# First input quarter and first weight blocks from DRAM arrays that are contiguous per transfer

## The chip, the cores and the metric

The kernel runs on one core of one Trainium2 chip. The metric is device time in microseconds of one execution, as the median of several runs. A second number, the span, runs from the first to the last instruction in the profile of one execution.

## The reference

One layer on a sequence of 1024 vectors of width 1024, all in float32:

```python
h = x @ w_in + b_in                       # -> xa | za | xb | zb | ga | gb, 1024 columns each
ya = RG_LRU(causal_conv4(xa)) * silu(za)
yb = MultiScalePool(xb) * silu(zb)
y  = (sigmoid(ga) * (ya @ w_proj_a) + sigmoid(gb) * (yb @ w_proj_b)) @ w_out + b_out
x  = LayerNorm(alpha * x + y)
```

Nearly all arithmetic lies in matrix products: `x @ w_in` (1024 x 1024 x 6144), the gates of the RG-LRU, the pooling mix, the two projections and the output.

## The kernel before

Each float32 operand is split into a high part in a shorter float format (a CAST on ScalarE, names ending in h) and the low rest (a subtraction on VectorE, names ending in l). A product is then three matmuls: high x high, high x low, low x high (`passes`, L454). Most products are done by a Strassen-like scheme with seven instead of eight block products; its operands are sums of blocks that VectorE and DMA prepare.

The order on every engine is set by a planner (`Plan`, L162). The code first records all operations; `order` (L252) then gives TensorE its matmuls in recorded order, and every other engine the waiting operation that is due first, by costs and due times of its own. All recorded operations are emitted from L388, so in the profile nearly everything has line 388 and is told apart by the names of its tiles.

What concerns the change is the start (L952 to L1022). Six warm-up matmuls on a tile of zeros (`ps_warm`) occupy TensorE while the first data come in. The first group of `w_in` is two blocks of columns, 0 and 1, whose product is done plainly, without the seven-product scheme; its results are the banks `ps_s`. The contraction of 1024 is cut into four quarters q = 0 to 3. Each quarter has two input tiles `xr[q][0]` and `xr[q][1]` of 128 partitions x 1024 (512 KB), loaded from the array `xq`, which the host has already arranged so that one such tile is one contiguous stretch, 4 KB per partition.

The first quarter is loaded in five pieces (`dma_x`, L978): of tile 0 columns 0 to 255, 256 to 511 and 512 to 1023, and of tile 1 its two halves. All are issued by SyncE (SP). The weights of the first group lie in tiles `w0r` (one per block, 128 x 1024). They are loaded by `dma_w0` (L971) in seven pieces: those of quarter 0 in three (64, 64 and 128 KB), issued by ScalarE (ACT), then quarter 1 and quarters 2 and 3 of each block, issued by SyncE. The source is `w_in[block]`, in which a partition has 4 KB: eight runs of 128 numbers (512 bytes), and a piece takes one, two or four of them. In a quarter the two halves kh = 0 and 1 are four runs apart, so a piece that takes both halves reads two separate runs per partition.

After that `split_w0` and `split_x` cast and subtract piece by piece, and `mm0` (L996) multiplies. On ScalarE the order is: its three DMA issues, a table load, the cast of the first input piece, the cast of the first weight piece, and so on.

Of the kernel before, what the change touches and what calls it, by code (L numbers as in the profile page):

```python
# [11 lines left out]
F32 = mybir.dt.float32  # L12
F32R = mybir.dt.float32r
# [3 lines left out]
P = 128  # L17
S = 1024
D = 1024
NK = D // P  # L20
H = 512
# [376 lines left out]


@with_exitstack  # L400
def layer_kernel(ctx: ExitStack, tc: tile.TileContext, xq, x, w_in, par, wg, w_pool, wpa, wpb, w_out, rows, out):
    nc = Plan(tc)

    def pool(name, bufs, space=None):
# [16 lines left out]
    def wt(name, dt=F32R, shape=(P, 2, H)):  # L421
        return wpool.tile(list(shape), dt, tag="w", name=name)
# [4 lines left out]
    def kt(name, dt=F32):  # L427
        return kpool.tile([P, S], dt, tag="k", name=name)

    def et(name):  # L430
        return epool.tile([P, H], F32, tag="e", name=name)

    def bank(name):
        return psum.tile([P, H], F32, tag="ps", name=name)
# [4 lines left out]
    out = Ref(result, as_strided(Ref.base, [S, D], [D, 1]))  # L439
    HALF = [slice(0, H), slice(H, S)]  # L440
    V, A = nc.vector, nc.scalar
# [8 lines left out]
    def split(raw, hi, lo):  # L450
        A.copy(hi, raw)
        V.tensor_tensor(lo, raw, hi.bitcast(F32), ALU.subtract)

    def passes(ps, w, m, first, last):  # L454
        (wh, wl), (mh, ml) = w, m
        for i, (a, b) in enumerate(((wh, mh), (wh, ml), (wl, mh))):
            nc.tensor.matmul(ps, a, b, start=first and i == 0, stop=last and i == 2, skip_group_check=True)
# [9 lines left out]
    KQ = 4  # L467
# [127 lines left out]
    order = [("G", 0)]  # L595
# [4 lines left out]
    def blocks_of(kind, c):  # L600
        if kind == "A":
            return XA + c, ZA + c
        if kind == "B":
            return XB + c, ZB + c
        sec = GA if c < 4 else GB
        return sec + c % 4, sec + c % 4 + 4
# [297 lines left out]
    def b_pool(g):  # L904
# [15 lines left out]
        if g == 1:  # L920
# [5 lines left out]
    sp, m, nl, y, z, z2, acc = (const.tile([P, 8], F32, name=n)  # L926
                                for n in ("sp", "sp_m", "sp_nl", "sp_y", "sp_z", "sp_z2", "sp_acc"))
# [28 lines left out]
    psw = bank("ps_warm")  # L956
    for i in range(WARM):
        nc.tensor.matmul(psw, warm[:, 0:P], warm, start=True, stop=True)
    first = blocks_of(*order[0])
    wr, wh, wl = [[f(f"{t}{n}") for n in range(2)] for t, f in  # L960
                  (("w0r", lambda n: wt(n, F32)), ("w0h", wt), ("w0l", wt))]

    xr = [[kt(f"xr{q}_{i}", F32) for i in range(2)] for q in range(KQ)]
    x13 = [[xt(f"x13{t}{q}") for t in "hl"] for q in range(KQ)]
    x2 = [xt(f"x2_{q}") for q in range(KQ)]
    xb = [xt(f"xb_{q}") for q in range(KQ)]

    def w0_part(t, n, a, b):
        return t[n].rearrange("p h (k m) -> p h k m", m=P)[:, :, a:b, :]

    def dma_w0(n, a, b, h=slice(0, 2)):  # L971

        (A if a == 0 else nc.sync).dma_start(w0_part(wr, n, a, b)[:, h], w_in[first[n]].rearrange("p (h k) m -> p h k m", h=2)[:, h, a:b, :])

    def split_w0(n, a, b, h=slice(0, 2)):
        split(*(w0_part(t, n, a, b)[:, h] for t in (wr, wh, wl)))

    def dma_x(q, i, sl=slice(0, S)):  # L978
        nc.sync.dma_start(xr[q][i][:, sl], xq[q, i][:, sl])


    def quarter(q, kh, h):
        if kh == h:
            return x13[q][0][:, kh, :], x13[q][1][:, kh, :]
        t = x2[q] if kh else xb[q]
        return t[:, 0, :], t[:, 1, :]
# [7 lines left out]
    ps0 = [[bank(f"ps_s{n}_{h}") for h in range(2)] for n in range(2)]  # L994

    def mm0(q, kh, h, n, cs=slice(0, H)):  # L996
        sl = slice(q * P, (q + 1) * P)
        passes(ps0[n][h][:, cs], (wh[n][:, kh, sl], wl[n][:, kh, sl]), tuple(t[:, cs] for t in quarter(q, kh, h)),
               q == 0 and kh == h and cs.start == 0, q == KQ - 1 and kh != h)


    PARTS = [slice(0, H // 2), slice(H // 2, H)]
    dma_w0(0, 0, 1, slice(0, 1))
    with nc.within(-2 * SOON):
        for sl in PARTS:
            dma_x(0, 0, sl)
    dma_w0(0, 0, 1, slice(1, 2))
    dma_w0(1, 0, 1)
    dma_x(0, 0, HALF[1])
    dma_x(0, 1, HALF[0])  # L1010
    dma_x(0, 1, HALF[1])
    dma_w0(0, 1, 2)
# [53 lines left out]
    def parts(q, n=0):  # L1066
        r = xr[q][0].rearrange("p (i s) -> p i s", i=2)
        todo = [(r, *x13[q])] + [(xr[q][raws[p][0]][:, HALF[raws[p][1]]], *quarter(q, *p)) for p in ((0, 1), (1, 0))]
        for raw, t, u in todo[n:]:
            hi(raw, t)  # L1070
        for raw, t, u in todo[n:]:
            lo(raw, t, u)
        for kh, h in ((0, 0), (1, 1), (0, 1), (1, 0)):
            for n in range(2):
                mm0(q, kh, h, n)

    def each(f, qs, *a):
        for q in qs:
            f(q, *a)

    split_w0(0, 0, 1, slice(0, 1))
    for kh, h in ((0, 0), (1, 1), (0, 1), (1, 0)):
        if kh == h == 1:
            split_w0(0, 0, 1, slice(1, 2))
        for sl in PARTS if kh == h == 0 else (slice(0, H),):
            split_x(0, kh, h, sl)
            mm0(0, kh, h, 0, sl)
        if kh == h == 1:
            split_w0(1, 0, 1)
            mm0(0, 0, 0, 1)  # L1090
        if kh or h:
            mm0(0, kh, h, 1)
# [29 lines left out]
    g = Group("A0", w.out, X, *takes0)  # L1122
# [44 lines left out]
    for i in range(1, len(order)):  # L1167
# [17 lines left out]
        if i > 1:  # L1185
            g = Group(f"{kind}{c}", W.pop(i), X, *takes)
# [170 lines left out]
    for i, (n, j) in enumerate(steps):  # L1357
# [7 lines left out]
        if j == 1:  # L1365
            a, c, m1, um = [[None] * KQ for _ in range(4)]
        X_, W_ = ([(hi_[:, k, :], lo_[:, k, :]) for hi_, lo_ in ops[i][o:o + 2] for k in range(2)] for o in (0, 2))
        for g in range(KQ):
# [5 lines left out]
            for q in range(KQ):  # L1374
                sl = slice(q * P, (q + 1) * P)
# [10 lines left out]
            if (n, j) in DONE:  # L1386
                d, h = DONE[n, j]
                d += g
                if j == 3:
                    t, u = ps, et(f"c12_{n}{g}") if n == "b" else None  # L1390
                else:
                    t = u = m1[g] if j == 2 else um[g][:, HALF[h]]
# [12 lines left out]
            if (n, j, g) in CASTS:  # L1405
                k = CASTS.index((n, j, g))
# [89 lines left out]
    a, c = ([None] * KQ for _ in range(2))  # L1496
# [25 lines left out]
    for g in range(KQ):  # L1522
        o_product(c[g], 4, g, False, True)
        o_add(4 + g, 1, c[g], -1, False, True)
        pieces = (slice(0, H),) if g < KQ - 1 else (slice(0, H // 2), slice(H // 2, H))
# [60 lines left out]
```

## Time and profile before

| | us |
|---|---|
| median of 3 runs | 740.91 (740.2 to 741.23) |
| the profiled execution | 740.07 |
| its span | 738.3 |
| TensorE busy (matmuls) | 729.5 |
| VectorE busy | 600.8 |
| ScalarE busy | 459.0 |
| GpSimd busy | 67.9 |

In the rows of the profile PE is TensorE, PEld its weight loads, DVE is VectorE, ACT ScalarE, POOL GpSimd and SP SyncE; SPq and ACTq are these engines' issues of DMAs. A timeline row has the start, the length, the engine, the line, the operation and out<-in. A bracket holds the idle time ahead of it and what ended that. Matmuls are pipelined, and their ends are modelled: the distance between starts is what one costs. `w0r<-in_w_in` is a load of weights of the first group, `xr<-in_xq` one of the input.

### The profile page before, as it was taken

The numbers are of one execution on the slowest core, as the hardware profiler recorded it, in microseconds if no ns is written. First come the engines' busy times: TensorE is split into PE (matmuls) and PEld (weight loads), VectorE is DVE, ScalarE is ACT, GpSimd is POOL, SyncE is SP. The second block draws the span as 40 slices with busy tenths as digits, with TensorE's granted clock in tenths as the row PEclk, the third lists the DMA queues.
The fourth block names the chain that finished last, engine by engine and source line by source line (L and its number), as shares of the span: only waits on it lengthen the run. The fifth ranks groups of instructions, "written<-read, shape, count | busy, mean of one in ns | idle before, by whom it ended". The sixth has DMA issues, their size and how long they took to land.

```text
span 738.3 us, 8785 instructions
## 1 busy us (share of the span) xinstructions
PE 729.5 (99%) x3249; PEld 599.4 (81%) x3249; DVE 600.8 (81%) x741; ACT 459.0 (62%) x587; POOL 67.9 (9%) x119
## 2 busy tenths in 40 slices
PE   9999999999999999999999999999999999999996
PEld 7887888888787878788888888888888888888885
DVE  7999796969696878977986768879948786999686
ACT  7686959686877868688844445447553545315473
POOL 0171011111101111100011100100000000000021
PEclk9999999999999999999999999999999999999999
DMA  9247979588988989842187954999679996758748
GB/s 320 111 142 198 264 180 279 135 240 224 303 161 217 328 206 282 219 113 91 54 204 154 212 114 158 278 315 331 235 241 303 311 333 234 267 201 232 196 80 149
DMA packets 64227, 158.98 MB, mean 215 GB/s; under 512 B 4340, under 2 KB 8308, under 8 KB 64120
## 3 DMA queue, kind: packets, MB, share of 16 engines
q1 hardware_dynamic: 43512, 106.26, 41.4%
q0 software_dynamic: 20112, 51.91, 33.6%
q8 instruction: 25, 0.41, 0.2%
q10 hardware_dynamic: 560, 0.26, 0.1%
q14 instruction: 18, 0.15, 0.1%
HBM read 137.43 MB, written 77.07 MB: 291 GB/s over the span
## 4 chain that ended last, share of the span: by engine, by line
PE 99%; DVE 1%; DVEq 0%; issue 0%
PE a_A L388 11%; PE a_B L388 11%; PE a_G L388 11%; PE oa L388 6%; PE pa_a L388 6%; PE pa_b L388 6%; PE c_B L388 6%; PE c_A L388 6%; PE c_G L388 5%; PE ps_s L388 3%; PE oc L388 3%; PE pc_b L388 3%; PE pc_a L388 3%; PE ps_pool L388 3%; PE e_B L388 3%; PE e_A L388 3%
## 5 line engine op out<-in xcount | busy, mean ns | idle before, releaser
L388 ACT ACT_TABLE_LOAD x38 | 48.8, 1283 | 3.0 <-issue 2.3
L388 DVE TENSOR_TENSOR i<-i,xc 128x1024 f32<-128x1024 f32 x8 | 9.8, 1225 | 26.9 <-ACT i L388 26.9
L388 DVE SCALAR_TENSOR_TENSOR xc<-xp,par_sb,xc 128x1023 f32<-128x1023 f32 (+2 forms) x24 | 30.7, 1281 | 0.5
L388 PE MATMUL pa_a<-oh,oh 128*128 128x512 f32 x64 | 24.9, 389 | 0.0
L388 PE MATMUL pa_a<-ol,oh 128*128 128x512 f32 x64 | 24.9, 389 | 0.0
L388 PE MATMUL pa_a<-oh,ol 128*128 128x512 f32 x64 | 24.9, 389 | 0.0
L388 PE MATMUL pa_b<-oh,oh 128*128 128x512 f32 x64 | 24.9, 389 | 0.0
L388 PE MATMUL pa_b<-ol,oh 128*128 128x512 f32 x64 | 24.9, 389 | 0.0
L388 PE MATMUL pa_b<-oh,ol 128*128 128x512 f32 x64 | 24.9, 389 | 0.0
L388 ACT ACTIVATE zb<-zb,par_sb 128x1024 f32<-128x1024 f32 (+1 forms) x16 | 15.0, 938 | 14.2 <-DVE zb L388 14.1
L388 ACT ACTIVATE r<-ps_g,par_sb 64x512 f32<-64x512 f32 x32 | 21.9, 683 | 2.1 <-DVE rb_B L388 0.8
L388 ACT ACTIVATE i<-ps_g,par_sb 64x512 f32<-64x512 f32 x32 | 21.9, 684 | 1.9 <-DVE r L388 1.4
L388 PE MATMUL c_A<-x64h,wd_A 128*128 128x512 f32 x64 | 21.0, 389 | 0.0
L388 PE MATMUL c_B<-x64h,wd_B 128*128 128x512 f32 x64 | 21.0, 389 | 0.0
L388 POOL DMA_DIRECT2D out<-y x7 | 8.5, 1210 | 130.0 <-ACT sd L388 117.4
L388 PE MATMUL ps_pool<-mixh,wp 128*128 128x512 f32 x64 | 20.3, 389 | 0.0
L388 PE MATMUL e_A<-x,wah_A 128*128 128x512 f32 x64 | 19.7, 389 | 0.0
L388 PE MATMUL e_B<-x,wah_B 128*128 128x512 f32 x64 | 19.7, 389 | 0.0
L388 POOL COPY paced<-pace 128x1 f32<-128x1 f32 x17 | 6.4, 376 | 130.9 <-ACT pace L388 130.9
L388 PE MATMUL c_G<-x64h,wd_G 128*128 128x512 f32 x56 | 18.4, 389 | 0.0
L388 DVE TENSOR_TENSOR_SCAN r<-a,i 128x1024 f32<-128x1024 f32 x8 | 18.3, 2284 | 0.1
L388 PE MATMUL e_G<-x,wah_G 128*128 128x512 f32 x56 | 17.2, 389 | 0.0
(521 smaller groups left out, 2534.5 us busy)
## 6 DMA issues: line engine op xcount, KB each, us to landing
sg<-sg SPq DMA_DIRECT2D x16, 512.0 KB, 4.3
ra_A<-in_w_in SPq DMA_DIRECT2D x8, 512.0 KB, 7.1
rb_A<-in_w_in SPq DMA_DIRECT2D x8, 512.0 KB, 7.5
xb<-bias SPq DMA_DIRECT2D x4, 1024.0 KB, 12.8
ya<-r SPq DMA_DIRECT2D x8, 512.0 KB, 5.7
xb<-in_x POOLq DMA_DIRECT2D x4, 1024.0 KB, 8.8
ra_B<-in_w_in SPq DMA_DIRECT2D x8, 512.0 KB, 4.3
rb_B<-in_w_in SPq DMA_DIRECT2D x8, 512.0 KB, 6.6
```

Source lines behind the costliest of these rows:

```text
L388: getattr(getattr(nc, t.op[0]), t.op[1])(*a, **k)
```

## The change

The host builds two further input arrays. `x0` holds the five pieces of the first input quarter one behind the other, each stored so that its 128 partitions follow each other without a gap (1 or 2 KB per partition). `w0` holds the seven pieces of the first group's weights in the same manner (512 bytes, 1 KB or 2 KB per partition). `xq` keeps quarters 1 to 3. The loads of the pieces read from the new arrays; their number, sizes, issuing engines and destination tiles remain.

For the weights the layout within a partition of SBUF changes with it: from halves, quarters, columns (`p h (k m)`) to quarters, halves, columns (`p k h m`), so that a piece is one run there too. `split_w0` and `mm0` take the new indices. A 128-column block remains one run.

```diff
-    wr, wh, wl = [[f(f"{t}{n}") for n in range(2)] for t, f in
-                  (("w0r", lambda n: wt(n, F32)), ("w0h", wt), ("w0l", wt))]
+    wr, wh, wl = [[wt(f"{t}{n}", dt, (P, KQ, 2, P)) for n in range(2)] for t, dt in
+                  (("w0r", F32), ("w0h", F32R), ("w0l", F32R))]
...
-    def w0_part(t, n, a, b):
-        return t[n].rearrange("p h (k m) -> p h k m", m=P)[:, :, a:b, :]
+    pieces = {}
+    for src0, shapes in ((x0, [(P, H // 2)] * 2 + [(P, H)] * 3), (w0, [(P, 1, h, P) for h in (1, 1, 2)] + [(P, 1, 2, P)] * 2 + [(P, 2, 2, P)] * 2)):
+        at = 0
+        for shape in shapes:
+            names = " ".join("pkhm"[-len(shape):]) if len(shape) == 4 else "p s"
+            size = int(np.prod(shape))
+            piece = src0[at:at + size].rearrange(f"({names}) -> {names}", **dict(zip(names.split(), shape)))
+            pieces.setdefault(id(src0), []).append(piece)
+            at += size
...
-        (A if a == 0 else nc.sync).dma_start(w0_part(wr, n, a, b)[:, h], w_in[first[n]].rearrange("p (h k) m -> p h k m", h=2)[:, h, a:b, :])
+        i = {0: (n + h.start if n == 0 else 2), 1: 3 + n, 2: 5 + n}[a]
+        (A if a == 0 else nc.sync).dma_start(wr[n][:, a:b, h], pieces[id(w0)][i])
...
-        nc.sync.dma_start(xr[q][i][:, sl], xq[q, i][:, sl])
+        from_ = xq[q - 1, i][:, sl] if q else pieces[id(x0)][{(0, 0): 0, (0, H // 2): 1, (0, H): 2, (1, 0): 3, (1, H): 4}[i, sl.start]]
+        nc.sync.dma_start(xr[q][i][:, sl], from_)
...
+    w0 = w_blocks[[32, 36]].reshape(2, P, 2, 4, P).transpose(0, 1, 3, 2, 4)
...
+        "x0": np.concatenate([xq[0, i][:, a:b].ravel() for i, a, b in ((0, 0, H // 2), (0, H // 2, H), (0, H, S), (1, 0, H), (1, H, S))]),
+        "w0": np.concatenate([w0[n][:, a:b, h:g].ravel() for n, a, b, h, g in (
+            (0, 0, 1, 0, 1), (0, 0, 1, 1, 2), (1, 0, 1, 0, 2), (0, 1, 2, 0, 2), (1, 1, 2, 0, 2), (0, 2, 4, 0, 2), (1, 2, 4, 0, 2))]),
```

No engine gets another sequence of instructions. What stands at the start of ScalarE's row, before (-) and now (+); `in_w_in` and `in_w` are the source arrays, `w0r` the weight tiles of the two blocks:

```order
-L388 DMA w0r_87<-in_w_in 128x128 x2
-L388 DMA w0r_106<-in_w_in 128x2x128
+L1595 UNCONDITIONAL_BRANCH
+L388 DMA w0r_87<-in_w 128x128 x2
+L388 DMA w0r_106<-in_w 128x256
 L388 ACT_TABLE_LOAD
 L388 CAST x13h_142<-xr_0_89 128x256
```

The two loads of block 0 and the one of block 1 stand where they stood, ahead of the table load; the third now moves one run of 256 numbers per partition instead of two runs of 128.

More of the change, by code (lines that the diff above doesn't have):

```diff
@@ L400, in layer_kernel @@
 @with_exitstack
-def layer_kernel(ctx: ExitStack, tc: tile.TileContext, xq, x, w_in, par, wg, w_pool, wpa, wpb, w_out, rows, out):
+def layer_kernel(ctx: ExitStack, tc: tile.TileContext, xq, x, x0, w0, w_in, par, wg, w_pool, wpa, wpb, w_out, rows, out):
     nc = Plan(tc)
@@ L958, in layer_kernel @@
         nc.tensor.matmul(psw, warm[:, 0:P], warm, start=True, stop=True)
-    first = blocks_of(*order[0])
-    wr, wh, wl = [[f(f"{t}{n}") for n in range(2)] for t, f in
-                  (("w0r", lambda n: wt(n, F32)), ("w0h", wt), ("w0l", wt))]
+    wr, wh, wl = [[wt(f"{t}{n}", dt, (P, KQ, 2, P)) for n in range(2)] for t, dt in
+                  (("w0r", F32), ("w0h", F32R), ("w0l", F32R))]
     xr = [[kt(f"xr{q}_{i}", F32) for i in range(2)] for q in range(KQ)]
@@ L966, in layer_kernel @@
     xb = [xt(f"xb_{q}") for q in range(KQ)]
-    def w0_part(t, n, a, b):
-        return t[n].rearrange("p h (k m) -> p h k m", m=P)[:, :, a:b, :]
+    pieces = {}
[7 more added lines that the diff above has]
+            at += size
     def dma_w0(n, a, b, h=slice(0, 2)):
-        (A if a == 0 else nc.sync).dma_start(w0_part(wr, n, a, b)[:, h], w_in[first[n]].rearrange("p (h k) m -> p h k m", h=2)[:, h, a:b, :])
+        i = {0: (n + h.start if n == 0 else 2), 1: 3 + n, 2: 5 + n}[a]
+        (A if a == 0 else nc.sync).dma_start(wr[n][:, a:b, h], pieces[id(w0)][i])
     def split_w0(n, a, b, h=slice(0, 2)):
-        split(*(w0_part(t, n, a, b)[:, h] for t in (wr, wh, wl)))
+        split(*(t[n][:, a:b, h] for t in (wr, wh, wl)))
     def dma_x(q, i, sl=slice(0, S)):
-        nc.sync.dma_start(xr[q][i][:, sl], xq[q, i][:, sl])
+        from_ = xq[q - 1, i][:, sl] if q else pieces[id(x0)][{(0, 0): 0, (0, H // 2): 1, (0, H): 2, (1, 0): 3, (1, H): 4}[i, sl.start]]
+        nc.sync.dma_start(xr[q][i][:, sl], from_)
     def quarter(q, kh, h):
@@ L996, in mm0 @@
     def mm0(q, kh, h, n, cs=slice(0, H)):
-        sl = slice(q * P, (q + 1) * P)
-        passes(ps0[n][h][:, cs], (wh[n][:, kh, sl], wl[n][:, kh, sl]), tuple(t[:, cs] for t in quarter(q, kh, h)),
+        passes(ps0[n][h][:, cs], (wh[n][:, q, kh, :], wl[n][:, q, kh, :]), tuple(t[:, cs] for t in quarter(q, kh, h)),
                q == 0 and kh == h and cs.start == 0, q == KQ - 1 and kh != h)
@@ L1562 @@
     rows = np.stack([np.asarray(b_out[0]), np.asarray(ln_gain[0]), np.asarray(ln_bias[0])])
+    w_blocks = blocks(w_in[0])
+    w0 = w_blocks[[32, 36]].reshape(2, P, 2, 4, P).transpose(0, 1, 3, 2, 4)
     xt = x2.T.reshape(2, 4, P, 2, H)
     xq = np.stack([np.stack([xt[0, :, :, 0], xt[1, :, :, 1]], axis=2), np.stack([xt[0, :, :, 1], xt[1, :, :, 0]], axis=2)], axis=1)
+    xq = np.ascontiguousarray(xq).reshape(4, 2, P, S)
     arrays = {
-        "xq": np.ascontiguousarray(xq).reshape(4, 2, P, S),
+        "xq": xq[1:],
         "x": np.ascontiguousarray(x2),
-        "w_in": blocks(w_in[0]),
+        "x0": np.concatenate([xq[0, i][:, a:b].ravel() for i, a, b in ((0, 0, H // 2), (0, H // 2, H), (0, H, S), (1, 0, H), (1, H, S))]),
+        "w0": np.concatenate([w0[n][:, a:b, h:g].ravel() for n, a, b, h, g in (
+            (0, 0, 1, 0, 1), (0, 0, 1, 1, 2), (1, 0, 1, 0, 2), (0, 1, 2, 0, 2), (1, 1, 2, 0, 2), (0, 2, 4, 0, 2), (1, 2, 4, 0, 2))]),
+        "w_in": w_blocks,
         "par": par,
```

## The prediction

> **What bounds the kernel now.** I read the page first, then the chain that ended last in order of time, and then the timelines of the first ten microseconds, since the change touches nothing after them. The page gives TensorE nearly the whole span:
>
> ```profile
> span 738.3 us, 8785 instructions
> ...
> PE 729.5 (99%) x3249; PEld 599.4 (81%) x3249; DVE 600.8 (81%) x741; ACT 459.0 (62%) x587; POOL 67.9 (9%) x119
> ```
>
> A busy share can hide small holes, so the chain matters more. Columns are start, length, what ran and how many:
>
> ```profile
> 1.44 2.93 PE ps_warm L388 x6
> 4.38 23.75 PE ps_s L388 x99
> 28.13 2.72 PE a_A L388 x12
> ...
> 728.07 2.88 PE oe L388 x24
> ```
>
> The chain is TensorE from 1.44 to 730.95 us. Twelve matmuls of 512 columns take 2.72 us, so one takes 0.227 us; that is the pace of full speed here. No transfer ends a wait of TensorE anywhere after the first quarter. Hence the change can only move the moment at which this train of matmuls gets going; whatever it wins there should arrive at the end unchanged, unless a later operand then comes too late. The beginning of the train, as the timeline of TensorE has it:
>
> ```profile
> 3.31 1.05 PE L388 MATMUL ps_warm<-warm 128*128 128x512 f32 x2
> 4.38 0.58 PE L388 MATMUL ps_s<-x13h,w0h 128*128 128x256 f32 x1
> 4.77 0.46 PE L388 MATMUL ps_s<-x13l,w0h 128*128 128x256 f32 x1
> 5.03 0.41 PE L388 MATMUL ps_s<-x13h,w0l 128*128 128x256 f32 x1
> 5.24 0.41 PE L388 MATMUL ps_s<-x13h,w0h 128*128 128x256 f32 x1
> 5.45 0.41 PE L388 MATMUL ps_s<-x13l,w0h 128*128 128x256 f32 x1
> ...
> 5.88 0.67 PE L388 MATMUL ps_s<-x13h,w0h 128*128 128x512 f32 x1
> 6.47 0.79 PE L388 MATMUL ps_s<-x13l,w0h 128*128 128x512 f32 x1
> 7.07 0.63 PE L388 MATMUL ps_s<-x13h,w0l 128*128 128x512 f32 x1
> 7.49 0.44 PE L388 MATMUL ps_s<-x13h,w0h 128*128 128x512 f32 x1
> 7.77 0.40 PE L388 MATMUL ps_s<-x13l,w0h 128*128 128x512 f32 x1
> 8.01 0.40 PE L388 MATMUL ps_s<-x13h,w0l 128*128 128x512 f32 x1
> ```
>
> Ends are modelled, so I read distances between starts. Two things show. First, 256 columns take 0.21 us (5.24 to 5.45), so 512 take 0.43: about half of full pace. The step from 7.77 to 8.01 is 0.24; full pace begins near 7.6. Second, there are four holes. The two warm-up matmuls from 3.31 are through at about 3.31 + 2 x 0.43 = 4.17, and the first real one starts at 4.38: 0.21. From 4.38 to 4.77 is 0.39 instead of 0.21: 0.18. From 5.88 to 6.47 is 0.59 instead of 0.43: 0.16. From 6.47 to 7.07 is 0.60 instead of 0.43: 0.17. That is 0.72 us in all, the most that better feeding could give, and it is time at half pace.
>
> Which of these holes wait for a transfer is told by ScalarE (which rounds each piece to its high part) and VectorE (which takes the rest):
>
> ```profile
> 0.72 1.55 ACTq L388 DMA_DIRECT2D w0r<-in_w_in  x3
> 2.30 1.28 ACT L388 ACT_TABLE_LOAD   x1 [2.30 <-issue]
> 3.73 0.41 ACT L388 CAST x13h<-xr 128x256 fp32r<-128x256 f32 x1
> 4.04 0.29 ACT L388 CAST w0h<-w0r 128x128 fp32r<-128x128 f32 x1
> ...
> 5.08 0.62 ACT L388 CAST x13h<-xr 128x512 fp32r<-128x512 f32 x1 [0.17 <-DMA xr<-in_xq]
> 5.60 0.40 ACT L388 CAST w0h<-w0r 128x256 fp32r<-128x256 f32 x1
> ```
>
> ```profile
> 5.73 0.69 DVE L388 TENSOR_TENSOR x13l<-xr,x13h 128x512 fp32r<-128x512 f32 x1 [0.36 <-ACT x13h L388]
> ```
>
> The table load ends at 2.30 + 1.28 = 3.58, and the first cast starts at 3.73. Elsewhere in the trace an operation follows its table load at once:
>
> ```profile
> 59.83 1.28 ACT L388 ACT_TABLE_LOAD   x1
> 61.12 1.15 ACT L388 ACTIVATE z<-z,par_sb 128x1024 f32<-128x1024 f32 x1
> ```
>
> There it is 0.01 us. So some 0.14 us before 3.73 is the first input piece still on its way. The third piece holds ScalarE for 0.17 at 5.08, and through VectorE's x13l (5.73 + 0.69 = 6.42) this makes the hole at 6.47. The hole at 4.77 is the chain from cast to subtraction to TensorE; no transfer is in it.
>
> **The change part by part.** No instruction changes its place on an engine. The loads of the first quarter and of the first group's weights keep their number, bytes and queues; only their sources become one stretch each. These rows show what issuing costs now:
>
> ```profile
> 0.72 0.39 SPq L388 DMA_DIRECT2D xr<-in_xq  x1
> 1.63 0.43 SPq L388 DMA_DIRECT2D xr<-in_xq  x1
> 3.94 0.33 SPq L388 DMA_DIRECT2D xr<-in_xq  x1
> 4.32 0.67 SPq L388 DMA_DIRECT2D w0r<-in_w_in  x1
> 1.17 0.45 ACTq L388 DMA_DIRECT2D w0r<-in_w_in  x1
> 1.65 0.62 ACTq L388 DMA_DIRECT2D w0r<-in_w_in  x1
> ```
>
> The load at 3.94 is a whole 128x1024 tile, already one stretch: 0.33. Pieces of a row cost 0.39 to 0.45, and the weights taken in two runs per partition 0.62 to 0.67. I put every changed issue between 0.33 and its present price. ScalarE's three then take about 3 x 0.33 + 2 x 0.04 = 1.07 instead of 1.55, so its table load may end 0.48 earlier, at 3.10; then the landing alone decides the first cast.
>
> First term, the first matmul. The first piece is issued 0.39 - 0.33 = 0.06 sooner, and behind it less is read in short runs. At best the first matmul follows the warm-up directly (0.21 sooner), at worst the landing stays (0). I take 0.1, nearer to the 0.06 that a row shows.
>
> Second term, the hole at 6.47. The third piece is issued from 1.63 to 2.06; with the two issues ahead of it cheaper by 0.06 and about 0.1, and its own by 0.1, its issue ends 0.26 sooner. If it also lands 0.26 sooner, the cast starts at 4.82, x13l ends at 6.16, and TensorE, which is ready at 5.88 - 0.1 + 0.43 = 6.21, no longer waits: it is there 0.26 sooner than 6.47. The extra 0.17 behind this hole looks like a weight load laid bare by it and would go too: 0.43. But the engines move data here at what looks like their limit, which speaks against a full gain:
>
> ```profile
> 3.00:4.00 1.00, 1.00 (x4) 0.55 (x2) 0.00 (x0) 0.86 (x2) 0.00 (x0) 1.00 1.10 380
> ```
>
> The last columns are the share of the DMA engines (1.10) and GB/s (380). I take both terms together as 0.3 at the matmul of 7.07, with ends 0 and 0.43.
>
> Third, from half pace to the end of the kernel. If full pace begins at the same moment, 0.3 us more of half-pace work is worth 0.3 x 0.227/0.43 = 0.16; if it begins earlier with the work, all 0.3 remains. I take 0.2, with ends 0 and 0.43. The Trainium skill (TensorE: Matmul & The Clock Gate, section "Part 1: The HAM clock gate") has a free-running activity window decide when the pace doubles, not the start of the kernel; by that the sum is 0.16. The trace agrees that the pace doubles once, but cannot show what decides it.
>
> Edits that cost nothing. The weight tiles are kept in another order within a partition; their casts become 128x256 instead of two runs of 128, and the present 128x256 input cast (0.41) is as long as the present two-run cast of w0h (0.40). Each 128-column weight block remains one run for TensorE. Later operands have room for a train that is 0.2 to 0.4 us earlier. The tightest that I find is the low part of xb:
>
> ```profile
> 7.81 0.69 DVE L388 TENSOR_TENSOR xb<-xr,xb 128x512 fp32r<-128x512 f32 x1
> 8.93 0.62 PE L388 MATMUL ps_s<-xb,w0h 128*128 128x512 f32 x2
> ```
>
> It is done at 8.50, and the second of the two matmuls, which uses it, starts at 8.93 + 0.23 = 9.16: 0.66 us of room.
>
> The sum: the profiled execution took 740.07 us, of which 738.3 is the span and 1.77 lies around it, which nothing here changes. 740.07 - 0.2 = 739.9. The median of the runs is 740.91, 0.84 above that execution; 740.91 - 0.2 = **740.7 us**.
>
> **The rivals.** (1) The transfers land no sooner: the wait is a fixed latency and not the layout. For it: the first piece is needed at 3.73, 3.01 us after its issue began, and only 0.39 of this is the issue. Against it: shorter issues at least shift what is queued behind. Result 740.9. The Trainium skill (DMA: Bandwidth & Descriptors, section "Anatomy of one DMA") speaks for this rival: it gives a fit, taken on the GpSimd path, of about 2.0 us fixed plus bytes over 436 GB/s; 131 KB would be an estimated 2.3 us, most of it untouched by any layout. The 3.01 us here agree only in size.
>
> (2) Fewer holes bring full pace forward. Work from 4.38 to 7.49 is 3.11 us at half pace and would take 3.11 x 0.227/0.43 = 1.64 at full pace, so at most 1.47 is won, 1.7 with the first term: 739.2. For it: full pace comes only when TensorE has run a while without large holes. Against it: the holes left by VectorE remain. The same section of TensorE: Matmul & The Clock Gate gives a window of 3.4 us, an estimated 1.7 us if one window is saved.
>
> (3) Slower: a small stretch of 64 to 128 KB that all sixteen engines read at once is delivered worse than the same bytes spread over 4 KB rows, and the first input piece lands late. Place: the first cast, at 3.73. Each microsecond delays TensorE by as much. Alone it passes 0.2% at 1.48 us, a first cast after 5.2; but an idle TensorE also may defer full pace, by up to another such stretch (1.47), and then half a microsecond is nearly enough. With 0.7 late and most of the other: 0.7 + 1.2 = 1.9, 742.8. For it: nothing in the rows. Against it: the contiguous loads in this trace have the cheapest issues, and the engines' limit is met with any layout.
>
> **How the numbers follow.** Forecast 0.72, rival 1 0.18, rival 2 0.05, rival 3 0.05. About 0.2% (1.48 us) is what a measurement of this kernel can tell from no change. The forecast and rival 1 lie inside it, and so does part of rival 2: faster 0.03, same 0.93, slower 0.04. The runs of before lie 0.71 below to 0.32 above their median. With a gain of 0 to 0.43 this gives 740.2 - 0.43 = 739.8 at the low end, and 741.23 with 0.2 for a single late landing at the high end: 739.8 to 741.4. Rivals 2 and 3 lie outside.
>
> **What would show it.** Right: issues of w0r near 0.33, ScalarE's table load ending near 3.1, a first cast before 3.73 and a first real matmul between 4.17 and 4.38, the matmul of 6.47 near 6.2, then 2.72 us per twelve to the end. A first cast at 3.73 or later shows rival 1 or 3; a step to full pace well before 7.4 rival 2. The forecast is wrong if the median leaves 739.8 to 741.4, or if the issues keep their prices.

## The result, and the profile after

The changed kernel takes 741.93 us (median of 22 runs, 740.24 to 743.56); the kernel before took 740.57 beside it (22 runs, 739.94 to 741.78). The ratio is 1.0015, with a 95% interval of 1.0008 to 1.0021: slower, by about 1.1 us (the medians lie 1.36 apart, the means 1.16), where 0.2 us less had been forecast. The median lies outside the range given. The spread has grown too, from 1.8 to 3.3 us.

The profiled execution took 740.43 us, 0.36 more than that of before. The page:

```profile
span 738.7 us, 8785 instructions
...
PE 729.2 (99%) x3249; PEld 599.1 (81%) x3249; DVE 600.9 (81%) x741; ACT 459.0 (62%) x587; POOL 68.2 (9%) x119
```

The busy times are those of before. The chain that ended last, in order of time (start, length, what), goes at its beginning:

```profile
1.63 4.30 DMA xr<-in_x
...
5.95 0.63 ACT x13h L388
...
6.60 0.70 DVE x13l L388
...
7.35 4.86 PE ps_s L388 x20
```

And where the first group ends, in the same view of the whole span:

```profile
7.35 21.18 PE ps_s L388 x92
28.53 2.72 PE a_A L388 x12
```

Before, this chain held the warm-up matmuls and then only TensorE. Now it begins with a transfer: the third input piece, issued at 1.63 as before, takes 4.30 us, and TensorE waits for it. From `a_A` on nothing differs but the offset: 28.53 instead of 28.13, and the last group, `oe`, starts at 728.47 instead of 728.07. Whatever the change does is done within the first 28 us. ScalarE tells which piece is late:

```profile
0.72 1.38 ACTq L388 DMA_DIRECT2D w0r<-in_w  x3
2.13 1.28 ACT L388 ACT_TABLE_LOAD   x1 [2.13 <-issue]
3.42 0.41 ACT L388 CAST x13h<-xr 128x256 fp32r<-128x256 f32 x1
...
4.56 0.40 ACT L388 CAST x13h<-xr 128x256 fp32r<-128x256 f32 x1 [0.53 <-DMA xr<-in_x]
...
5.95 0.62 ACT L388 CAST x13h<-xr 128x512 fp32r<-128x512 f32 x1 [0.79 <-DMA xr<-in_x]
```

The first piece is there earlier: its cast starts at 3.42 instead of 3.73, straight after the table load. The second holds ScalarE for 0.53 us, and the third is cast at 5.95 instead of 5.08, after 0.79 us of waiting instead of 0.17. TensorE follows:

```profile
4.17 0.49 PE L388 MATMUL ps_s<-x13h,w0h 128*128 128x256 f32 x1
...
5.48 0.58 PE L388 MATMUL ps_s<-x13l,w0h 128*128 128x256 f32 x1
5.85 0.32 PE L388 MATMUL ps_s<-x13h,w0l 128*128 128x256 f32 x1
6.62 0.50 PE L388 MATMUL ps_s<-x13h,w0h 128*128 128x512 f32 x1 [0.45 <-ACT x13h L388]
7.35 0.50 PE L388 MATMUL ps_s<-x13l,w0h 128*128 128x512 f32 x1 [0.23 <-DVE x13l L388]
7.68 0.40 PE L388 MATMUL ps_s<-x13h,w0l 128*128 128x512 f32 x1
7.92 0.39 PE L388 MATMUL ps_s<-x13h,w0h 128*128 128x512 f32 x1
```

The first real matmul comes 0.21 sooner (4.17), the one that stood at 6.47 comes 0.88 later (7.35). Yet only 0.40 reaches the end, because in this execution full pace (0.23 us per 512 columns) is there right after the hole, where before it began near 7.6. So this profiled execution is a lucky one, 1.5 us below its kernel's median.

The DMA engines' rate, in stretches of one microsecond; the last two columns are their share and GB/s. After:

```profile
2.00:3.00 1.00, 1.00 (x4) 0.77 (x3) 0.00 (x0) 0.87 (x1) 0.00 (x0) 1.00 0.99 292
3.00:4.00 1.00, 1.00 (x4) 0.55 (x2) 0.14 (x1) 0.99 (x3) 0.00 (x0) 1.00 1.04 201
4.00:5.00 1.00, 1.00 (x4) 0.76 (x3) 0.49 (x3) 0.47 (x3) 0.00 (x0) 1.00 0.89 262
```

And two of these stretches before; 3.00 to 4.00 stood at 380:

```profile
2.00:3.00 1.00, 1.00 (x4) 0.77 (x3) 0.00 (x0) 0.70 (x1) 0.00 (x0) 1.00 0.83 191
...
4.00:5.00 1.00, 0.98 (x3) 0.62 (x3) 0.83 (x3) 0.91 (x4) 0.00 (x0) 1.00 1.07 282
```

The transfers begin faster (292 against 191 GB/s) and then fall to 201 where they had run at 380, with the engines' share at 1.04: over this microsecond the engines are occupied, but deliver little. In quarters of a microsecond the dip is sharper, and in its deepest quarter the engines are busy for only half of the time:

```profile
3.25:3.50 0.25, 0.25 (x2) 0.18 (x1) 0.00 (x0) 0.24 (x2) 0.00 (x0) 1.00 1.21 156
3.50:3.75 0.25, 0.25 (x3) 0.15 (x1) 0.00 (x0) 0.25 (x2) 0.00 (x0) 1.00 0.50 90
```

### The profile page after: what moved, and what is told of

Its sections match the earlier page's. It is cut to its first block, busy times and chain, and to the rows that moved or that the text cites. A ratio compares the mean times of both kernels' runs of the same rounds, so it can differ in the third digit from the quotient of the medians.

```text
span 738.7 us, 8785 instructions
## 1 busy us (share of the span) xinstructions
PE 729.2 (99%) x3249; PEld 599.1 (81%) x3249; DVE 600.9 (81%) x741; ACT 459.0 (62%) x587; POOL 68.2 (9%) x119
## 4 chain that ended last, share of the span: by engine, by line
PE 98%; DMA 1%; DVE 1%; SPq 0%; DVEq 0%; ACT 0%; issue 0%
PE a_A L388 11%; PE a_B L388 11%; PE a_G L388 11%; PE oa L388 6%; PE pa_a L388 6%; PE pa_b L388 6%; PE c_B L388 6%; PE c_A L388 6%; PE c_G L388 5%; PE oc L388 3%; PE pc_b L388 3%; PE pc_a L388 3%; PE ps_pool L388 3%; PE e_B L388 3%; PE e_A L388 3%; PE ps_s L388 3%
```

## The experiments

Two questions are open: what makes the third piece late, and what its lateness costs. The first theory was that contiguity itself does it: small stretches, read by all engines at once, are delivered worse after the first of them. Its rivals: that the weights' new layout does it, or the input's, or that pieces lie next to each other, or that the two streams lie in another place to each other. On the cost, the theory is that the hole ahead of the third piece is passed on, and that the time at which TensorE reaches full pace decides the rest. All ratios are against the kernel before, with 95% intervals; the times of casts and landings in a kernel come from its one profiled execution.

**Input alone, weights alone, weights as one run but in rows.** e1_x_only keeps the weights as they were, e2_w_only the input; they are the change with the other half undone. e3_w_pitch gives the weights' partition the new order, so that each piece is one run per partition, but leaves the 4 KB rows:

```diff
-        (A if a == 0 else nc.sync).dma_start(w0_part(wr, n, a, b)[:, h], w_in[first[n]].rearrange("p (h k) m -> p h k m", h=2)[:, h, a:b, :])
+        (A if a == 0 else nc.sync).dma_start(wr[n][:, a:b, h], w0[n][:, a:b, h])
...
+    w0 = w_blocks[[32, 36]].reshape(2, P, 2, 4, P).transpose(0, 1, 3, 2, 4)
```

> Only the five pieces of the first input quarter come from the new array x0; the weights are loaded as before. Theory A (a small contiguous stretch, read by all DMA engines at once, is served slowly, and the input pieces are what TensorE waits for): the third input piece lands some 4.0 us or more after its issue begins (before 3.4, after 4.3), its cast starts at 5.5 or later (before 5.08, after 5.95), and the median is 0.7 to 1.5 us over before. Theory B (the weight loads, no longer cut into short runs, take the DMA engines away from the input pieces): as before within 0.4 us, third piece 3.4. Theory C (the new order within the weight tiles in SBUF): as before.

> Only the weights of the first group come from the new array w0, with the new order in SBUF; the input is loaded as before. Theory A: the weight pieces may land later, but the third input piece lands near 3.4 to 3.8 us, and the median is within 0.5 us of before. Theory B: third piece at 4.0 or more, median 0.7 to 1.5 us over before. Theory C: the same 0.7 to 1.5 over before.

> The weights come from an array of their own in which each partition keeps a row of 4 KB, so that a piece is one run per partition but no contiguous stretch; the order in SBUF is the new one, and the input is loaded as before. Theory A: as before within 0.4 us, no stretch in it anywhere. Theory B: if the longer runs per partition are what takes the engines away, 0.7 to 1.5 us over before, like the kernel with only the weights contiguous. Theory C: also 0.7 to 1.5 over before.

| | ratio | first cast | third cast | third: issue to landing |
|---|---|---|---|---|
| before | 1 | 3.73 | 5.08 | 3.4 |
| after | 1.0015 [1.0008, 1.0021] | 3.42 | 5.95 | 4.3 |
| e1_x_only | 1.0010 [1.0001, 1.0018] | 3.61 | 5.88 | 4.6 |
| e2_w_only | 1.0006 [0.9997, 1.0015] | 3.47 | 5.75 | 4.1 |
| e3_w_pitch | 0.9998 [0.9989, 1.0007] | 3.65 | 5.22 | 3.6 |

Either half alone makes the third piece late, even the weights, though the piece itself is then read as before; the first theory had it at 3.4 to 3.8 there. The time of e2_w_only can't be told from that of before, its late piece notwithstanding: its interval includes 1. Neither one run per partition nor the new order in SBUF is to blame, since e3 has both. ScalarE in e3_w_pitch, for the waits:

```profile
3.65 0.40 ACT L388 CAST x13h<-xr 128x256 fp32r<-128x256 f32 x1 [0.23 <-DMA xr<-in_xq]
...
5.22 0.62 ACT L388 CAST x13h<-xr 128x512 fp32r<-128x512 f32 x1 [0.44 <-DMA xr<-in_xq]
```

**An extra load, first try.** e4_late adds to the kernel before a 256 KB load ahead of the third piece, to make that piece late without a new layout:

```diff
+    with nc.within(-2 * SOON):
+        nc.sync.dma_start(xr[3][0][:, HALF[0]], xq[3, 0][:, HALF[0]])
```

> The kernel before, with one more load of 256 KB (into a part of a later input tile, which is loaded again in its turn) issued ahead of the third input piece, so that this piece and all behind it land some 0.7 to 0.9 us later. It prices lateness alone. If late input pieces are the whole cause, and cost only the holes that they make, the median is 0.4 to 1.0 us over before. If holes also put off the moment of full pace in some executions, it is 1.0 to 2.0 us over, with single runs 2.5 or more over. If lateness is hidden, as before.

747.36 us, ratio 1.009 [1.0076, 1.0104]. This is a miss: the planner saw the new operation and put other operations into another order as well, so the 6.6 us are not the price of lateness alone (there is a further hole of 2.56 us at 29). It is done cleanly below.

**The loads by themselves.** e5_bursts runs only the first loads, 40 times, from one array: input and weights each in rows (r), contiguous (c), or contiguous with 2 MB from piece to piece (a).

> The loads by themselves: the kernel computes nothing of the layer, it only loads, 40 times over, a burst like the first one of the kernel (five input pieces on SyncE, three weight pieces on ScalarE, the same sizes), each burst after all of the last has landed, and writes a tile to the output. Five kinds of burst in turn, eight of each, from fresh places of one array: rr (input and weights from 4 KB rows, as before), cc (both contiguous, the pieces one behind the other, as after), cr and rc (only input, only weights contiguous), aa (each piece contiguous, the pieces 2 MB apart). Theory A (contiguous stretches are served slowly): the third input piece lands 0.5 to 0.9 us later in cc than in rr in most bursts, cr and rc lie between. If one short stretch read by all engines is the reason, aa is as cc; if neighbouring pieces disturb each other, aa is as rr. Rival (lateness in the kernel has to do with its start, or with the two arrays, and not with the layout): all five kinds agree within 0.2 us.

Mean landings of the five input pieces, us after SP's first issue. A landing is taken as the moment at which VectorE begins to copy four columns of the piece; it copies the pieces in their order:

| input, weights | 1 | 2 | 3 | 4 | 5 |
|---|---|---|---|---|---|
| rows, rows | 2.49 | 3.12 | 5.61 | 6.33 | 7.07 |
| contiguous, contiguous | 2.33 | 2.85 | 5.41 | 6.06 | 6.71 |
| contiguous, rows | 2.34 | 2.87 | 5.92 | 6.53 | 7.17 |
| rows, contiguous | 2.53 | 3.13 | 5.52 | 6.21 | 6.83 |
| apart | 2.34 | 2.92 | 5.39 | 6.02 | 6.66 |

The third piece is late in all five kinds, in rows too. Here contiguity on both sides makes nothing worse (5.41 against 5.61), contiguous input alone does a little (5.92), and the first theory is in trouble; but the bursts differ from the kernel in two ways, one array instead of two and no loads behind.

**Pieces apart, a filled hole, a clean late piece.** e6_apart puts each piece of the changed kernel 1 MB from the next:

```diff
-            at += size
+            at += 262144
```

e7_fill puts one matmul on the zero tile into the changed kernel's hole, by a hook that emits it at its place and leaves the planner unaware of it; e8_late does e4's extra load with the same hook, and all other instructions stay where they were:

```diff
+            if kh == h == 1:
+                nc.before[len(nc.tasks)] = lambda: [nc.tc.nc.tensor.matmul(psw.place(), warm[:, 0:P].place(), warm.place(), start=True, stop=True) for _ in range(1)]
```

```diff
+    nc.before[len(nc.tasks)] = lambda: nc.tc.nc.sync.dma_start(xr[3][0][:, HALF[0]].place(), xq[3, 0][:, HALF[0]])
```

> The changed kernel with every piece still one contiguous stretch, but the pieces 1 MB apart in their arrays. If a short stretch read by all engines is slow, it stays 0.5 to 1.5 us over before, with the third input piece at 4.0 us or more. If neighbouring pieces disturb each other, it falls to within 0.4 us of before, third piece near 3.4 to 3.6.

> The changed kernel with one more matmul on the tile of zeros (512 columns), put between the two first input pieces' products and those of the third piece, where TensorE is idle; every other engine keeps its order. It does no useful work, so if the holes cost only their own length, the time stays that of the changed kernel or is up to 0.4 us more. If holes also put off the moment of full pace by a whole activity window in some executions, those executions become rarer: the median falls by 0.4 to 1.2 us from the changed kernel's, to within 0.5 us of before, and the slowest runs (743 and more) are gone.

> The kernel before, with one more load of 256 KB issued ahead of the third input piece on SyncE and nothing else changed in any engine's order (in the earlier kernel of this kind the planner had also turned two casts round). It prices lateness alone: the third piece should land about 0.7 us later and the two behind it too. If late input pieces are the cause of the loss, the median is 0.7 to 1.6 us over before, as for the changed kernel, with a wider spread of the runs. If lateness of this size is hidden, within 0.3 us of before.

e6: 741.85, ratio 1.0014 [1.0004, 1.0024], third cast at 6.52. That the pieces are neighbours is not the cause. e7: 742.14, ratio 1.0012 [1.0003, 1.0021]: one filler brings nothing to the median, which was to fall by 0.4 to 1.2 from the changed kernel's if the filler kept the pace up. None of its 11 runs takes 743 or more (the highest is 742.72), as that case would have it, but with 4 of the changed kernel's 22 up there this can be chance. Its loads are those of the changed kernel, and yet its third cast stands at 6.50 instead of 5.95: the landing itself varies by half a microsecond. e8: 743.63, ratio 1.0038 [1.0025, 1.0050], third cast at 6.98: with the layout of before, one more load ahead of the third piece, which makes it and the pieces behind it late, makes the kernel 2.9 us slower. That is more than the 0.7 to 1.6 put down for this case, and the piece is later than in the changed kernel, too. TensorE in e8_late shows where more than the hole comes from:

```profile
7.65 0.50 PE L391 MATMUL ps_s<-x13h,w0h 128*128 128x512 f32 x1 [1.84 <-ACT x13h L391]
8.37 0.80 PE L391 MATMUL ps_s<-x13l,w0h 128*128 128x512 f32 x1 [0.23 <-DVE x13l L391]
8.97 0.63 PE L391 MATMUL ps_s<-x13h,w0l 128*128 128x512 f32 x1
9.39 0.63 PE L391 MATMUL ps_s<-x13h,w0h 128*128 128x512 f32 x1
...
11.52 0.39 PE L391 MATMUL ps_s<-x13h,w0l 128*128 128x512 f32 x1
11.75 0.63 PE L391 MATMUL ps_s<-xb,w0h 128*128 128x512 f32 x2
```

After the hole the steps of 512 columns are 0.42 (8.97 to 9.39), half pace, until 11.52, and 0.23 from there. The granted clock (the third column from the right) has the same, in stretches of one microsecond of e8_late:

```profile
7.00:8.00 1.00, 0.35 (x1) 0.19 (x1) 0.37 (x1) 1.00 (x3) 0.00 (x0) 1.00 0.97 369
8.00:9.00 1.00, 0.78 (x3) 0.53 (x3) 1.00 (x3) 0.97 (x2) 0.00 (x0) 0.54 1.02 384
9.00:10.00 1.00, 1.00 (x4) 0.81 (x3) 1.00 (x2) 0.28 (x1) 0.00 (x0) 0.50 1.17 390
10.00:11.00 1.00, 1.00 (x4) 0.81 (x3) 1.00 (x3) 1.00 (x3) 0.00 (x0) 0.50 0.95 377
11.00:12.00 1.00, 1.00 (x5) 0.73 (x5) 1.00 (x3) 0.67 (x3) 0.00 (x0) 0.75 1.01 391
```

A value of 0.54 means 0.92 us at half clock, one of 0.75 means 0.50: in all 0.92 + 1 + 1 + 0.50 = 3.4 us. In e7_fill, where the hole is 1.33 us in spite of the filler, the row is 0.84, 0.50, 0.50, 0.50, 0.95 from 8 to 13: 0.32 + 3 + 0.10 = 3.4 us again. The Trainium skill (TensorE: Matmul & The Clock Gate, section "Part 1: The HAM clock gate") says that the pace is decided over a free-running window of 3413 ns; both traces agree in the length. So a hole costs itself, and now and then one such stretch on top: 3.4 us at half clock do the work of 1.7, up to 1.7 us more. The stretch begins 0.4 us after the hole's end in e8 and 1.5 us after it in e7.

**Loads by themselves, nearer to the kernel.** e9_bursts2 repeats the bursts with input and weights in two arrays and with the kernel's next loads behind them.

> The loads by themselves again, now with the three loads that follow in the kernel, with the input and the weights in two arrays, and with the weights of before as they were (two runs of 512 bytes per partition). It computes nothing of the layer. Kinds of burst, eight of each: rb (as before), cc (as after), cb (only input contiguous), rc (only weights contiguous), rr (weights in one run per partition from 4 KB rows). In the first such kernel the contiguous kinds brought the first piece 0.16 us sooner and the third not later than the rows did. If the layout alone makes the third piece late, rb and rr bring it 0.5 us or more sooner than cc, cb and rc. If lateness belongs to the kernel's start and not to the layout, all agree within 0.3 us again.

| input, weights | 1 | 2 | 3 (lowest to highest) | 4 | 5 |
|---|---|---|---|---|---|
| as before | 2.95 | 3.45 | 4.31 (4.25 to 4.41) | 5.97 | 6.89 |
| rows, one run in rows | 2.79 | 3.40 | 4.45 (4.16 to 5.28) | 6.41 | 7.09 |
| as after | 2.31 | 2.90 | 5.50 (5.02 to 6.05) | 6.29 | 6.93 |
| contiguous, as before | 2.27 | 3.11 | 5.32 (5.16 to 5.63) | 6.17 | 7.05 |
| rows, contiguous | 2.61 | 3.17 | 5.75 (5.27 to 6.19) | 6.41 | 7.15 |

Now the kernel's pattern is there, with nothing but loads, and the three kinds with something contiguous are the late ones, as the first theory has it. The first two pieces gain 0.55 to 0.64 us by the change, the third loses 1.2, and the fifth is where it was: the same bytes in the same time, handed out in another order. The kernel can use a first piece from 3.4 on, when ScalarE is through with its table load, and has a use for the third from about 4.9: it gets more of what it needs less.

**Which pieces.** e10_x_first makes only the first two input pieces contiguous, e11_x_rest only the other three; the weights are as before:

```diff
+        from_ = xq[q, i][:, sl] if q or not (i == 0 and sl.stop <= H) else pieces[{(0, 0): 0, (0, H // 2): 1, (0, H): 2, (1, 0): 3, (1, H): 4}[i, sl.start]]
```

> The kernel before with only the first two input pieces contiguous; the third to fifth and the weights come from rows. If a piece is late because it is itself a contiguous stretch, the third piece lands in about 3.4 to 3.6 us as before and the median is within 0.4 us of before. If the third is late because the first ones came faster (first cast before 3.65 instead of 3.73) and the engines ran dry or collide behind them, it takes 4.0 us or more, and the median is 0.5 to 1.3 us over before.

> The other half: the first two input pieces and the weights from rows, the third to fifth input piece contiguous. If a piece is late because it is itself a contiguous stretch, the third takes 4.0 us or more and the median is 0.5 to 1.3 us over before. If the fast first pieces are the cause, the third takes 3.4 to 3.6 and the median is within 0.4 us of before.

e10: 741.40, ratio 1.0010 [1.0001, 1.0019], third cast 5.55. e11: 742.00, ratio 1.0017 [1.0007, 1.0026], third cast 6.52. Either subset is enough. No single piece carries it.

**Rows, but one array.** e12_one_array is the kernel before, all in rows as it was, with the first quarter of the input and the two weight blocks copied into one array, the weights right behind the input. e13_bursts3 takes the loads alone, all in rows, and changes the distance and the loads behind.

```diff
-        (A if a == 0 else nc.sync).dma_start(w0_part(wr, n, a, b)[:, h], w_in[first[n]].rearrange("p (h k) m -> p h k m", h=2)[:, h, a:b, :])
+        (A if a == 0 else nc.sync).dma_start(w0_part(wr, n, a, b)[:, h], xw[2 + n].rearrange("p (h k m) -> p h k m", h=2, m=P)[:, h, a:b, :])
...
-        nc.sync.dma_start(xr[q][i][:, sl], xq[q, i][:, sl])
+        nc.sync.dma_start(xr[q][i][:, sl], (xq[q, i] if q else xw[i])[:, sl])
```

> The kernel before with its rows as they were, but the first input quarter and the first group's weights copied into one array, the weights right behind the input; no piece is contiguous. In the runs so far the first piece's cast started at 3.65 or later with the third piece 3.4 to 3.6 us after its issue, or at 3.61 or earlier with the third piece 3.9 to 4.9 us after its issue. If contiguity itself makes the third piece late: first cast at 3.65 to 3.75, third landing 3.3 to 3.7 us after its issue, cast at 5.0 to 5.3, ratio 0.999 to 1.001. If it is where the input and the weights lie to each other, as the one-array burst in rows suggested (first piece 2.49, third 5.61): first cast at 3.4 to 3.6, third landing 3.9 us or more after its issue, cast at 5.6 or later, ratio 1.001 to 1.002.

> Loads alone, the rest of the kernel left out: bursts of the first five input pieces and the weight pieces, all in rows, in five kinds of 8 bursts each: input and weights from two arrays with the follow-on loads behind them and without, weights 1 MB behind the input in the same array with and without follow-on loads, weights 12 MB away in the same array with follow-on loads. If the late third piece of the earlier one-array burst in rows (5.61 against 4.45 with two arrays and follow-on loads) came from where the two streams lie: the two kinds from two arrays at 4.3 to 4.6, the two at 1 MB at 5.3 to 5.9. If it came from the follow-on loads being absent: the two kinds without them at 5.3 to 5.9, those with them at 4.3 to 4.6, wherever the weights lie. In either case the first piece is 0.2 to 0.5 earlier in the kinds whose third is late, and the fifth is within 0.3 of 6.9 in all.

e12: 741.91 against 741.03, ratio 1.0008 [0.9999, 1.0017]. ScalarE and, below it, the rate:

```profile
3.60 0.40 ACT L388 CAST x13h<-xr 128x256 fp32r<-128x256 f32 x1
...
6.27 0.62 ACT L388 CAST x13h<-xr 128x512 fp32r<-128x512 f32 x1 [1.55 <-DMA xr<-in_xw]
```

```profile
2.00:3.00 1.00, 1.00 (x4) 0.77 (x3) 0.00 (x0) 0.69 (x1) 0.00 (x0) 1.00 0.96 307
3.00:4.00 1.00, 1.00 (x4) 0.55 (x2) 0.00 (x0) 0.99 (x3) 0.00 (x0) 1.00 0.97 195
```

Nothing is contiguous, and yet all the signs of the changed kernel are there: no wait ahead of the first cast, the third piece 1.55 us awaited, 307 and 195 GB/s. Its hole is 1.33 us, and the profiled execution lost its clock from 8.5 to 11.9. The interval of its ratio just includes 1, so whether it is slower in the mean stays unclear; the late landing does not.

e13, all in rows, means of 8 bursts each:

| where the weights lie | loads behind | 1 | 3 (lowest to highest) | 5 |
|---|---|---|---|---|
| another array | yes | 2.76 | 4.40 (4.07 to 5.25) | 7.00 |
| another array | no | 2.74 | 4.26 (4.13 to 4.51) | 6.35 |
| same array, 12 MB away | yes | 2.72 | 4.22 (4.07 to 4.37) | 7.00 |
| same array, 1 MB behind | yes | 2.49 | 5.99 (5.41 to 6.43) | 7.35 |
| same array, 1 MB behind | no | 2.46 | 5.61 (5.32 to 6.00) | 6.98 |

One burst with the weights in another array, as VectorE reads the pieces (what it waited for stands in the bracket):

```profile
112.17 2.23 SPq L52 DMA_DIRECT2D tfx<-in_xa  x5
...
114.99 0.17 DVE L61 COPY tfsink<-tfx 128x4 f32<-128x4 f32 x1 [2.78 <-DMA tfx<-in_xa]
...
116.37 0.17 DVE L61 COPY tfsink<-tfx 128x4 f32<-128x4 f32 x1 [0.83 <-DMA tfx<-in_xa]
```

And one with the weights 1 MB behind:

```profile
161.12 2.23 SPq L52 DMA_DIRECT2D nfx<-in_xa  x5
...
163.64 0.17 DVE L61 COPY nfsink<-nfx 128x4 f32<-128x4 f32 x1 [2.48 <-DMA nfx<-in_xa]
...
167.45 0.17 DVE L61 COPY nfsink<-nfx 128x4 f32<-128x4 f32 x1 [3.13 <-DMA nfx<-in_xa]
```

In these bursts what decides is where the weights lie; the same array as such is no matter, and the loads behind change little (0.14 and 0.38 us). This settles one more rival: with its first piece early, the changed kernel also issues its next load of 512 KB sooner (3.31 instead of 3.94), but in the bursts the third piece is late without any such load (5.61 in e5 and e13). So the first theory falls in its simple form: contiguity is one way to get a late third piece, and nearness of the two streams is another. What the late cases have in common, as far as these runs show, is only that the bytes which both queues read at once lie in other places of DRAM than before; not every new place does it (e3). Which addresses collide, if that is the reason, is not settled: pieces 1 MB apart (e6) are late, weights 12 MB away in rows are not, and contiguous weights far from the input (e2) are late again. Nor is it settled whether the fast beginning causes the slow middle, or both come from the placement: in every kernel and every kind of burst in which the first piece came early, the third came late, so no run separates the two.

## Why the prediction was wrong, point by point

**What bounds the kernel** was right: TensorE's train, with the offset set in the first 28 us and handed to the end unchanged (0.40 at `a_A`, 0.40 at `oe`). So was the warning that a later operand could come too late, but it was not followed up for the piece next in line.

**The issues** were priced wrong, without much effect. I put the changed ones at 0.33. ScalarE's three take 1.38 instead of 1.55 (1.07 expected), and the table load ends at 3.41, not 3.10. The input's issues kept their prices (0.72 and 1.63 are the first and the third piece):

```profile
0.72 0.39 SPq L388 DMA_DIRECT2D xr<-in_x  x1
1.63 0.43 SPq L388 DMA_DIRECT2D xr<-in_x  x1
```

The row of the 512 KB load did not carry over to pieces.

**First term, the first matmul**: right in direction, and at its upper bound. 0.1 expected, 0.21 found; the transfer did come sooner, and rival 1 falls.

**Second term, the hole at 6.47: this is the step that failed.** It put the end of the third piece's issue 0.26 sooner, worked the gain out from the case that it "also lands 0.26 sooner", and gave 0 as the worst case. It was issued at the same 1.63 and landed 0.9 later (4.3 us after its issue instead of 3.4); the matmul of 6.47 came at 7.35. The working moved the landing with the issue, as if a transfer's time did not depend on what the transfers ahead of it do. The sign of caution that it had, 380 GB/s as "what looks like their limit", was used only to shrink the gain: a burst at its limit that hands its first piece out earlier can hand a later one out later, and e9 shows that it does, with the last piece unmoved. A loss was not excluded by any row, so the bound of 0 should have been open downwards.

**Third term, the pace**: the way it was reckoned, a shift at half pace being worth something between half and all of itself, leaves out that a hole can cost a whole stretch of half pace, either by taking the full clock away again (e7, e8, e12) or by putting it off. A long hole is not needed for the latter: e10's is 0.27 us, e1's 0.58, and their profiled executions reach full pace only near 10.0 and 10.4, where that of before does so near 7.6. In e1_x_only:

```profile
6.55 0.80 PE L388 MATMUL ps_s<-x13h,w0h 128*128 128x512 f32 x1 [0.58 <-ACT x13h L388]
...
10.00 0.54 PE L388 MATMUL ps_s<-x13l,w0h 128*128 128x512 f32 x1
10.38 0.39 PE L388 MATMUL ps_s<-x13h,w0l 128*128 128x512 f32 x1
10.61 0.62 PE L388 MATMUL ps_s<-xb,w0h 128*128 128x512 f32 x2
```

e6_apart, which has the changed kernel's times (741.85; 740.27 to 743.62), was profiled at its slow end, 743.62, and there half pace lasts until 13.6:

```profile
11.07 0.63 PE L388 MATMUL ps_s<-x13h,w0l 128*128 128x512 f32 x1
11.49 1.05 PE L388 MATMUL ps_s<-xb,w0h 128*128 128x512 f32 x2
12.35 0.63 PE L388 MATMUL ps_s<-xb,w0l 128*128 128x512 f32 x1
```

Each run lists its mean granted clock, and so the changed kernel's 22 runs can be sorted, though only roughly. Four show 0.994, as the profiled executions of e7 (742.57) and e12 (742.32) do, which had the clock withdrawn; among 82 runs of the kernel before, in the experiments' comparisons, one does (742.45). A mean of 0.996 or 0.997 tells nothing alone, since runs of before at 740 to 741 us show it too; there the time has to sort. With one more at 0.996, the first kind took 742.01 to 742.60. Four took 743.37 to 743.56 at 0.997, as e6's profiled one with its late clock (743.62 at 0.997). The other thirteen have a mean of 741.10, the nine one of 742.79, and these nine put 9/22 x 1.69 = 0.7 us on the mean. Of 1.16 us of loss in the mean some 0.7 thus go with the stretches of half pace that the later piece sometimes brings. The other 0.5 is not the later piece alone: the profiled execution lost 0.4 with no further half pace, but e1's, at 741.76 and 0.998, had its full pace put off, and five of the thirteen lie at 741.4 to 742.1 with the same 0.998. How the loss divides is therefore not shown exactly. That the four belong to the same kind as e6's execution is argued from their times, since none of them was profiled.

**The rivals.** Rival 3 was right in its sign and its kind (a burst delivered worse, TensorE idle, full pace put off) and wrong in its place: it put the lateness at the first cast, 3.73, where the change helps, and said that nothing in the rows spoke for it. It was given 0.05. Its sum, 0.7 for the idle time and 1.2 for most of a stretch at half pace, has the two parts that were found, but as if every execution paid both: 742.8, against 741.93. Rival 2 did not occur as a mean; a single execution of the changed kernel can be as fast as 740.24.

**The price against the lateness.** Third cast and ratio, in order: 5.08 and 1; 5.22 and 0.9998; 5.55 and 1.0010; 5.75 and 1.0006; 5.88 and 1.0010; 5.95 and 1.0015; 6.27 and 1.0008; 6.50 and 1.0012 (e7, with its filler); 6.52 and 1.0014 and 1.0017; 6.98 and 1.0038. With intervals of about 0.0009 to either side, and a cast from one execution each, the order is not strict, but nothing with a cast after 5.5 is at or below 1. No version beats the kernel before measurably; e3_w_pitch equals it.

## What to carry to other kernels

Here a new DRAM layout did not make the burst of first loads shorter, it reordered the landings. Before such a change ask which piece the next engine waits for, and check that piece and not the first. The landing of a piece must not be moved along with its issue, and the bound of such a term stays open to both sides until a run shows it. What a late operand cost at the start was the hole and, in some executions, a further 3.4 us at half pace or a full pace that came 2.4 to 6 us later.

## What the runs showed of the hardware

Where two streams lie in DRAM changes the order of delivery by more than a microsecond: with the weights 1 MB behind the input in one array, the third piece landed 5.99 us after the first issue, with 12 MB between them 4.22 (e13); without the loads behind, it was 5.61 against 4.26 with the weights in another array. Over the microsecond of the dip the DMA engines count as busy (share 1.04 at 201 GB/s, and 1.10 at 380 before), so the busy share alone doesn't tell that a burst is well delivered; in its deepest quarter it falls to 0.50, at 90 GB/s.

A hole in a train of matmuls can take the full clock away again: in e8 (hole of 1.84 us), e7 (1.33) and e12 (1.33) the granted clock falls to 0.50 for 3.4 us. After 1.25 us in e11 it did not fall. Whether the length of the hole decides this or its moment is not shown. Before the first grant in a trace the column reads 1.00 although the starts stand 0.43 us apart; there only the distance of the starts shows half pace.
